# Attention and selection products on the full 128 x 128 array: operands of 4 to 64 rows, and results of 16 or 64 columns, widened with zeros

## The chip, the core and the metric

One core of a Trainium2 chip runs the whole program. The metric is the device time of one execution in microseconds (us); the lower, the better.

## The reference

Two transformer blocks on 512 tokens of 1024 features, in float32. Cut to what matters here:

```python
# block 1: forgetting attention (16 heads of 64) over 16 meta + 512 tokens, causal
logits = einsum('bhqd,bhkd->bhqk', qb, k) * scale + cb[..., None] - c[:, :, None, :]
p = softmax(where(allowed, logits, NEG)); y_a = einsum('bhqk,bhkd->bhqd', p, v)
# beside it retention: 4 heads, decayed scores, the same 16 + 512 keys; then gates, output products, SwiGLU

# block 2, two layers: neighbourhood attention (6 heads of 64: a window of the grid plus 256 context keys),
# grouped attention (6 query heads, 2 key heads of 64: 512 + 256 keys), a spatial gating unit, SwiGLU
s = concat([s_loc + bias, s_ctx], -1); p = softmax(s); o = p_loc @ v_win + p_ctx @ v_ctx
```

## The kernel before

Activations lie feature-major: a tile has 128 features on its 128 partitions and tokens along its columns. Where operands meet on TensorE they are pairs of float32r tiles (hi, lo) with hi + lo equal to the float32 value, and a product is made of three matmuls, hi hi, hi lo and lo hi (`mm3`, L296 to L303). A matmul takes a stationary operand (rows = what is summed over, columns = the rows of the result) and a moving one.

In the attention parts the head size is 64, half of the array's rows. A score is made of two matmuls instead of three. The first has all 128 rows: `A` holds the query's high part in 64 rows and its low part in the other 64, and `B1` holds the key's high part twice. The second has 64 rows: the query's high part against the key's low part, which lies in `B2`, one tile for both heads of a pair, in the head's own half:

```python
nc.tensor.matmul(ps[:, c:c + n], A[:, q], B1[:, c:c + n], start=True, stop=False)                  # L856
nc.tensor.matmul(ps[:, c:c + n], A[rows, q], B2[hp][rows, c:c + n], start=False, stop=True)        # L857
```

L856 and L857 are the forgetting attention (`fox`), L1476 and L1477 the neighbourhood attention (`na_streams`), L1655 and L1656 the grouped attention (`gqa`). After the scores come a maximum (VectorE), exponentials (ScalarE, into a tile `E`), transposes by TensorE (L892 in fox, L1330 in the other two), a split of the transposed tile in two (ScalarE writes `ph` at L322, then VectorE writes `pl` at L323), and the products with the values (L882 and L883; L1322). The other two add the reciprocal sums as a product with 64 result columns (L1339) in columns of the same bank.

Other operands with few rows: the meta tokens (16 keys: L882 and L883 with `VM`, the retention's `vmh` and `vml`) and constants that pick a row out of several (`esel`, `rsel`, `gsel`: 64 rows; L814, L815, L778 to L782, L1703). Results with 16 rows: transposes and scores of the 16 meta tokens.

The order of the work: generators are woven by a count of steps (`weave`), so that the projections of the next heads fill the attention of these; a scheduler then orders each engine's instructions, except GpSimd's, which keep the program's order. In block 2 an item of attention is 256 queries of one head; the scores of the next item go ahead of the sums of this one (`LOOK` is 1), and the values' product of a chunk of two key blocks comes one chunk after its transposes (`keysums`, L1311). Layer 0 has 18 items of either attention, layer 1 has 12. `E` has 5 buffers in the grouped attention and 6 in the neighbourhood attention (`EBUFS`, `NEBUFS`). While attention runs, GpSimd makes the low parts of the weights (`wlo`, L271).

Of the kernel before, what the change touches and what calls it, by code (L numbers as in the profile page):

```python
# [18 lines left out]
KD = 8  # L19
# [12 lines left out]
# buffers  # L32
# [21 lines left out]
# tiles added up before a sum over partitions  # L54
# [4 lines left out]
# steps (or columns of products) that lie between an operand and its use  # L59
# [8 lines left out]
# the pace of the work beside the products  # L68
# [11 lines left out]
# columns of the packed per-feature vectors  # L80
# [49 lines left out]
class Kern:  # L130
    """The program. Where operands meet on the tensor engine they are float32r pairs (hi, lo) with
    hi + lo exactly the float32 value, and a product is hi hi + hi lo + lo hi."""
# [51 lines left out]
    def weave(self, fill, main, ahead=1.0):  # L184
        """Run two generators side by side so that they end together (fill sooner by `ahead`). Their
        numbers of steps come from the first trace. main may ask for steps of fill in self.fill."""
        i = len(self.counted)
        self.counted.append(None)
        nf, nm = self.counts[i] if self.counts else (1, 1)
        self.fill = fill = Steps(fill)  # L190
        im = 0
        for _ in main:
            im += 1
            while fill.live and (fill.n + 1) * nm <= im * nf * ahead:
                fill.step()
        while fill.live:
            fill.step()
        self.counted[i] = (max(fill.n, 1), max(im, 1))

# [13 lines left out]
    def pump(self, cols):  # L213
        """Let the queue keep pace with a product of so many columns."""
# [59 lines left out]
    def prefetch(self, n):  # L274
        """Load the first units of weights."""
# [3 lines left out]
    def wunit(self, name, idx, k0=0, k1=KD, width=128):  # L279
        """The next unit of weights, [128, k1 - k0, width] in two parts; later units are set going."""  # L280
# [15 lines left out]
    def mm3(self, pss, wh, wl, xhs, xls, start, stop):  # L296
        """pss += W^T X with W and X each in two parts; lists run over chunks of columns."""
# [22 lines left out]
    def split(self, hi, lo, src):  # L320
        """hi + lo = src exactly."""
# [4 lines left out]
    def rsqrt(self, v, w, side=False):  # L326
        """1/sqrt(v) for v [128, w] (w <= 40), to float32; with side set mostly on an engine that has time."""
# [4 lines left out]
        # a guess from the exponent, a step of third order (without its factor c = 3/8), one of second order  # L332
# [39 lines left out]
    def affine(self, v, st, toks, col0, a, b):  # L372
        """v = a st + b in the rows that the token tiles have."""
# [14 lines left out]
    def bcasting(self, r, toks, ps=None):  # L388
        """r [token, tile] to a PSUM tile whose rows are all r, tokens along columns. A generator."""
# [60 lines left out]
    def until(cnt, n):  # L450
        """Wait until so many tiles have been set going."""
# [3 lines left out]
    def rms1(self, X, U, gname, c0, n, acc=NACC):  # L455
        """U[:, c0:c0+n] = RMS norm of X over features, split. A generator."""
# [164 lines left out]
    def gates(self, ff, tri, room, chl):  # L621
        """chl = cumulative log sigmoid of the forget gates ff [head, token], split over two row groups."""
# [21 lines left out]
        # log sigmoid z = min(z, 0) - log1p(e), e = exp(-|z|); log1p(e) = 2 atanh(e / (2 + e))  # L644
# [26 lines left out]
    def rounded(self, T, name, shape):  # L671
        """A constant of zeros and ones as float32r."""
# [5 lines left out]
    def foxconsts(self, X, fc):  # L678
# [4 lines left out]
        esel, rsel = self.rounded(T, "esel", [64, 16]), self.rounded(T, "rsel", [64, 256])  # L683
# [3 lines left out]
        chl = T([64, 528], "chl", 1, F32R)  # L687
# [5 lines left out]
    def fox(self, X, Y, fx, mask, esel, rsel, kq, chl):  # L693
# [4 lines left out]
        for i in range(2):  # L698
            rt = T([64, 528], f"rt{i}", 1, F32R)
            nc.gpsimd.memset(rt.bitcast(F32), 0.0)  # L700
            rts.append(rt)
        raw, ready = {}, {}

        def proj(hp, first=False):
            """Projections of a pair of heads and the mean squares of q and k."""
# [6 lines left out]
            def stat(u, c0, n, sq):  # L712
                st = self.at()
                toks = [(i, a, m) for i, (a, m) in enumerate(self.TOK1) if c0 <= a < c0 + n]
                for x, (i, a, m) in enumerate(toks):        # sums of squares per token and head
                    nc.tensor.matmul(st[:m, 2 * x:2 * x + 2], sq[:, a - c0:a - c0 + m], self.hsel, start=True, stop=True)
# [44 lines left out]
        def pair(hp):  # L761
            """The operands of a pair's attention: q and k normalised, v by tokens."""
# [3 lines left out]
            # 1 / rms per token and head, in columns (q h0, q h1, k h0, k h1) per token tile  # L766
# [20 lines left out]
            B2[hp] = T([128, 528], "B2", 2, F32R)  # L787
# [3 lines left out]
        def values(hp):  # L791
# [3 lines left out]
            for i, (c, n) in enumerate(self.TOK1):  # L795
                o = pt[:, (i - 1) * 128:i * 128] if i else ptm[:16, 0:128]
                nc.tensor.transpose(o, vs[:, c:c + n], ident)
            VT, VM = T([128, 4, 2, 2, 64], "VT", 2, F32R), T([16, 2, 2, 64], "VM", 2, F32R)
# [3 lines left out]
            nc.scalar.activation(VM[:, :, 0, :], pmv, AF.Copy)  # L802
            nc.vector.tensor_tensor(VT[:, :, :, 1, :], ptv, VT[:, :, :, 0, :].bitcast(F32), op=ALU.subtract)
            nc.vector.tensor_tensor(VM[:, :, 1, :], pmv, VM[:, :, 0, :].bitcast(F32), op=ALU.subtract)
# [3 lines left out]
        def head(x):  # L808
            """A head's q and k in two parts, and its biases."""
            hp, h = divmod(x, 2)  # L810
            # bias +c (the scores carry the opposite sign), and with the causal mask
            pcb = self.mm()
            es = esel[:, x:x + 1].to_broadcast([64, 128])
# [15 lines left out]
            nc.vector.tensor_tensor(B2[hp][rows], ks[rows], B1[rows].bitcast(F32), op=ALU.subtract)  # L829
# [5 lines left out]
        def scores(x):  # L835
            hp, h = divmod(x, 2)
            A, B1, cb, cbm = ready.pop(x)
            rows = slice(64 * h, 64 * h + 64)
# [9 lines left out]
            for i in range(4):  # L848
# [23 lines left out]
        def sums(x):  # L872
# [6 lines left out]
            def pv():  # L879
                j, kp, n, ph, pl = todo.pop(0)  # L880
                vv = (VT[:, j, h] if j >= 0 else VM[:, h]).rearrange("p a d -> p (a d)")
                nc.tensor.matmul(py[:, 512 - n:512], vv, ph[:kp, :n], start=j < 0, stop=False)  # L882
                nc.tensor.matmul(py[:, 512 - n:512], vv, pl[:kp, :n], start=False, stop=j == 3)  # L883

            for j in range(-1, 4):
                n = 512 - 128 * max(j, 0)
                kp = 128 if j >= 0 else 16
# [6 lines left out]
                self.split(ph[:kp, :n], pl[:kp, :n], pe[:kp, :n])  # L894
                todo.append((j, kp, n, ph, pl))
# [8 lines left out]

        normed, B2, V, Es = {}, {}, {}, {}
# [20 lines left out]
    def retgates(self, X, Y, hs):  # L926
        """silu(g) = g (1 + tanh(g / 2)) / 2, the half being in hcol"""
# [10 lines left out]
    def ret(self, X, Y, rp):  # L938
# [10 lines left out]

        def proj(h):  # L950
            dec, decm = T([128, 512], "dec", 1), T([16, 512], "decm", 1)
            nc.scalar.dma_start(out=dec, in_=I["decay"][h])
            nc.scalar.dma_start(out=decm, in_=I["decaym"][h])
# [17 lines left out]
            # values, token-major, centred over the head's features  # L971
# [12 lines left out]
            for d in range(2):  # L984
                for i, (c, n) in enumerate(self.TOK1):
                    o = ptv[:, i - 1, d * 128:(d + 1) * 128] if i else ptm[:16, d * 128:(d + 1) * 128]
                    nc.tensor.transpose(o, vss[d][:, c:c + n], self.ident)
# [1064 lines left out]
```

## Time and profile before

| | us |
|---|---|
| median of 3 runs (3511.92 to 3517.06) | 3514.89 |
| span of the profiled execution, first to last instruction | 3506.6 |
| fox, 436 to 775 of the span | 339 |
| attention of layer 0, 1687 to 1965 | 278 |
| attention of layer 1, 2765 to 3012 | 247 |

The median is 8.3 us above the profiled execution's span: what lies around the span, with the difference between executions. PE is TensorE's matmuls, PEld its weight loads, DVE VectorE, ACT ScalarE, POOL GpSimd. "64\*128" in a row of PE is a matmul with 64 rows and 128 columns of stationary operand, "64x256" its moving operand. Matmuls overlap, so the pace of a stream is read from one start to the next and not from a matmul's own duration. A product of plain float32 operands (transposes, L1339) stands as two records.

### The profile page before, as it was taken

How to read it: one execution, taken by the hardware profiler on the slowest of the kernel's cores; microseconds unless marked ns; L12 is line 12 of the kernel's file. 1: busy time of each engine (PE TensorE's matmuls, PEld its weight loads, DVE VectorE, ACT ScalarE, POOL GpSimd, SP SyncE). 2: the span in 40 equal slices, each digit the busy share in tenths (PEclk: the TensorE clock that was granted, in tenths of full speed). 3: DMA queues.
4: the chain of work that ended last, by engine and by line, in shares of the span. 5: the costliest groups of instructions: out<-in, count | busy, mean ns of one | idle time of the engine just before them, and what ended most of it. 6: DMA issues, size and time to landing. Idle time of an engine off the chain costs nothing. (4 is left out here: it accounts for less than half of the span.)

```text
span 3506.6 us, 50184 instructions
## 1 busy us (share of the span) xinstructions
PE 3365.7 (96%) x19680; PEld 2907.4 (83%) x19680; DVE 2083.9 (59%) x4419; ACT 1324.2 (38%) x2273; POOL 481.8 (14%) x443
## 2 busy tenths in 40 slices
PE   8999999999999999999999989999998999989998
PEld 7999977878788987889677878888898777878887
DVE  7983577776633769764766674222256666674335
ACT  4222345552323523234554443111234464452223
POOL 0000122223200110011211240000013111230001
PEclk9999999999999999999999899999999999899999
DMA  6663421122133656643001222212234201334233
GB/s 206 212 201 95 138 68 49 37 64 62 63 98 106 197 171 197 193 143 99 23 16 55 68 82 91 67 61 61 73 112 131 67 20 54 93 115 125 88 99 103
DMA packets 112205, 350.89 MB, mean 100 GB/s; under 512 B 12896, under 2 KB 26784, under 8 KB 111712
## 3 DMA queue, kind: packets, MB, share of 16 engines
q1 hardware_dynamic: 86464, 280.07, 25.8%
q10 hardware_dynamic: 25216, 65.51, 5.8%
q8 instruction: 155, 2.54, 0.3%
q0 software_dynamic: 288, 2.10, 0.2%
q14 instruction: 82, 0.67, 0.1%
HBM read 339.24 MB, written 8.39 MB: 99 GB/s over the span
## 5 line engine op out<-in xcount | busy, mean ns | idle before, releaser
L269 ACT ACTIVATE whi<-raw 128x1024 fp32r<-128x1024 f32 (+3 forms) x543 | 550.1, 1013 | 1434.6 <-PE mm L301 783.1
L300 PE MATMUL mm<-ah,whi 128*128 128x512 f32 (+3 forms) x2496 | 809.3, 331 | 15.3 <-ACT s L546 6.8
L301 PE MATMUL mm<-al,whi 128*128 128x512 f32 (+3 forms) x2496 | 788.1, 327 | 1.3 <-DVE al L1157 1.0
L271 DVE TENSOR_TENSOR wlo<-raw,whi 128x1024 fp32r<-128x1024 f32 (+2 forms) x464 | 557.1, 1203 | 352.3 <-ACT whi L269 349.1
L303 PE MATMUL mm<-ah,wlo 128*128 128x512 f32 (+3 forms) x2496 | 715.3, 328 | 3.6 <-DVE wlo L271 3.6
L300 PEld LDWEIGHTS mm<-ah,whi 128*128 128x128 f32 x2496 | 474.4, 190 | 68.8 <-ACT ah L1156 7.8
L301 PEld LDWEIGHTS mm<-al,whi 128*128 128x128 f32 x2496 | 474.0, 190 | 42.3 <-DVE al L1157 3.1
L300 PE MATMUL at<-ah,whi 128*128 128x512 f32 (+4 forms) x1368 | 482.4, 354 | 7.8 <-DVE B L1439 2.2
L301 PE MATMUL at<-al,whi 128*128 128x512 f32 (+4 forms) x1368 | 459.1, 336 | 0.1
L303 PE MATMUL at<-ah,wlo 128*128 128x512 f32 (+4 forms) x1368 | 456.6, 335 | 0.0
L303 PEld LDWEIGHTS mm<-ah,wlo 128*128 128x128 f32 x2496 | 430.2, 190 | 31.1 <-DVE wlo L271 4.8
L300 PE MATMUL mm<-gh,whi 128*128 128x256 f32 (+3 forms) x1168 | 376.9, 327 | 0.9 <-ACT gh L322 0.6
L301 PE MATMUL mm<-gl,whi 128*128 128x256 f32 (+3 forms) x1168 | 367.7, 324 | 0.7 <-DVE gl L323 0.7
L303 PE MATMUL mm<-gh,wlo 128*128 128x256 f32 (+3 forms) x1168 | 339.5, 324 | 0.0
L300 PEld LDWEIGHTS at<-ah,whi 128*128 128x128 f32 x1368 | 264.8, 194 | 41.2 <-issue 10.8
L301 PEld LDWEIGHTS at<-al,whi 128*128 128x128 f32 x1368 | 265.5, 194 | 23.2 <-issue 3.2
L303 PEld LDWEIGHTS at<-ah,wlo 128*128 128x128 f32 x1368 | 264.0, 193 | 21.7 <-issue 0.7
L1119 POOL TENSOR_TENSOR sq<-x,x 128x256 f32<-128x256 f32 (+1 forms) x68 | 73.8, 1097 | 1252.5 <-DVE x L1176 819.1
L300 PEld LDWEIGHTS mm<-gh,whi 128*128 128x128 f32 x1168 | 220.6, 189 | 23.9 <-ACT gh L322 0.9
L301 PEld LDWEIGHTS mm<-gl,whi 128*128 128x128 f32 x1168 | 220.6, 189 | 18.0 <-DVE gl L323 1.4
L271 POOL TENSOR_TENSOR wlo<-raw,whi 128x1024 fp32r<-128x1024 f32 (+1 forms) x79 | 180.1, 2287 | 376.3 <-ACT whi L269 347.7
L550 DVE TENSOR_TENSOR s<-s,mm 128x256 f32<-128x256 f32 (+3 forms) x142 | 72.1, 527 | 240.5 <-PE mm L303 239.1
(385 smaller groups left out, 4873.8 us busy)
## 6 DMA issues: line engine op xcount, KB each, us to landing
raw<-in_wfin SPq DMA_DIRECT2D x116, 512.0 KB, 3.6
raw<-in_win SPq DMA_DIRECT2D x115, 512.0 KB, 3.6
wm<-in_wmod ACTq DMA_DIRECT2D x96, 512.0 KB, 4.2
raw<-in_w2in SPq DMA_DIRECT2D x52, 512.0 KB, 4.3
raw<-in_w1in SPq DMA_DIRECT2D x50, 512.0 KB, 4.0
raw<-in_wfout SPq DMA_DIRECT2D x48, 448.0 KB, 3.3
raw<-in_w1out SPq DMA_DIRECT2D x24, 448.0 KB, 3.4
raw<-in_w2out SPq DMA_DIRECT2D x24, 448.0 KB, 3.4
```

What stands on the lines that cost most here:

```text
L269: self.nc.scalar.activation(hi, raw, AF.Copy)
L271: eng.tensor_tensor(lo, raw, hi.bitcast(F32), op=ALU.subtract)
L300: t.matmul(ps, wh, xh, start=start, stop=False)
L301: t.matmul(ps, wh, xl, start=False, stop=False)
L303: t.matmul(ps, wl, xh, start=False, stop=stop)
L550: nc.vector.tensor_tensor(s[:, c], s[:, c], ps[1][:, 512 * b:512 * b + n], op=ALU.mult)
L1119: nc.gpsimd.tensor_tensor(x, X[j][:, c], X[j + 1][:, c], op=ALU.add)
```

## The change

Every operand with few rows gets all 128, the rest being zeros. `B2` becomes a tile for each half (`B2[h]`), whose other half GpSimd sets to zero once: for all pairs in fox and in the grouped attention; for the pairs 0 and 1 in the neighbourhood attention, where pair 2 writes into the tiles of pair 0. `VM`, `vmh`, `vml` and the meta tokens' decay become tiles of 128 rows, set to zero once. `esel`, `rsel`, `gsel`, `rt` and `chl` get 128 rows. Transposes, scores and sums of squares of the 16 meta tokens take 128 columns (the meta tokens and the 112 after them), and the product at L1339 has 128 result rows. Layer 0 gets 4 buffers of `E` in either attention (5 and 6 before; layer 1 keeps them), `yt` has one buffer instead of two, and a tile of zeros became one column. The number of matmuls is the same, 19077 in either program; VectorE and ScalarE have as many instructions as before.

```diff
-EBUFS = 5
-NEBUFS = 6
+EBUFS = (4, 5)
+NEBUFS = (4, 6)
...
+        B2 = [T([128, 528], f"B2{h}", 1, F32R) for h in range(2)]
+        VMs = [T([128, 2, 2, 64], f"VM{i}", 1, F32R) for i in range(2)]
+        for h in range(2):
+            nc.gpsimd.memset(B2[h][64 - 64 * h:128 - 64 * h].bitcast(F32), 0.0)
+            nc.gpsimd.memset(VMs[h].bitcast(F32), 0.0)
...
-                    nc.tensor.matmul(ps[:, c:c + n], A[rows, q], B2[hp][rows, c:c + n], start=False, stop=True)
+                    nc.tensor.matmul(ps[:, c:c + n], A[:, q], B2[h][:, c:c + n], start=False, stop=True)
...
-                nc.tensor.matmul(py[:, 512 - n:512], vv, ph[:kp, :n], start=j < 0, stop=False)
-                nc.tensor.matmul(py[:, 512 - n:512], vv, pl[:kp, :n], start=False, stop=j == 3)
+                nc.tensor.matmul(py[:, 512 - n:512], vv, ph[:, :n], start=j < 0, stop=False)
+                nc.tensor.matmul(py[:, 512 - n:512], vv, pl[:, :n], start=False, stop=j == 3)
...
-                    nc.tensor.transpose(pe[:kp, q0:q0 + 128], E[:, k0:k0 + kp], ident)
+                    nc.tensor.transpose(pe[:, q0:q0 + 128], E[:, k0:k0 + 128], ident)
...
-                nc.tensor.matmul(py[0:64, 256 + 128 * t:384 + 128 * t], rs[:, t:t + 1].to_broadcast([128, 64]),
+                nc.tensor.matmul(py[:, 256 + 128 * t:384 + 128 * t], rs[:, t:t + 1].to_broadcast([128, 128]),
                                  self.ident, start=False, stop=False)
...
-        yt = T([64, 256], "yt", 2)
+        yt = T([64, 256], "yt", 1)
...
-            B2 = self.xp.tile([128, T2], F32R, name=self.nm("B2"), tag="x", bufs=KD)
+            if pr < 2:
+                lows.append([self.nb2() if pr == 1 else self.xp.tile([128, T2], F32R, name=self.nm("B2"), tag="x", bufs=KD)
+                             for _ in range(2)])
+                for h in range(2):
+                    nc.gpsimd.memset(lows[pr][h][rows[1 - h]].bitcast(F32), 0.0)
+            B2 = lows[pr % 2]
...
-                            nc.tensor.matmul(o, A[rows, q], B2[rows, k0:k0 + 256], start=False, stop=True)
+                            nc.tensor.matmul(o, A[:, q], B2[h][:, k0:k0 + 256], start=False, stop=True)
...
-        B2 = self.xp.tile([128, T2], F32R, name=self.nm("gB2"), tag="x", bufs=KD)
         B = [keep([128, T2], "gB1", 2, F32R) for _ in range(2)]
+        B2 = [keep([128, T2], "gB2", 2, F32R) for _ in range(2)]
+        for g in range(2):
+            nc.gpsimd.memset(B2[g][64 - 64 * g:128 - 64 * g].bitcast(F32), 0.0)
...
-                    nc.tensor.matmul(ps[:, c:c + n], A[rows, q], B2[rows, k0 + c:k0 + c + n], start=False, stop=True)
+                    nc.tensor.matmul(ps[:, c:c + n], A[:, q], B2[kv][:, k0 + c:k0 + c + n], start=False, stop=True)
```

TensorE's queue in the grouped attention of layer 0, before: a tile of 128 queries' scores, then transposes. In these rows the shape is that of the result; `gB_15504` is `B1`, `gB_15503` the `B2` that both key heads share.

```order
L300 MATMUL at_16748<-ah_12064,whi_16634 128x512
L1655 MATMUL mm_16758<-gB_15504,A_16612 128x512
L1656 MATMUL mm_16758<-gB_15503,A_16612 128x512
L1655 MATMUL mm_16758<-gB_15504,A_16612 128x256
L1656 MATMUL mm_16758<-gB_15503,A_16612 128x256
L1330 MATMUL at_16766<-c_ident,E_16719 128x128
```

The same place in the change, where `gB_15491` is the key head's own `B2`:

```order
L300 MATMUL at_16740<-ah_12050,whi_16626 128x512
L1666 MATMUL mm_16750<-gB_15489,A_16601 128x512
L1667 MATMUL mm_16750<-gB_15491,A_16601 128x512
L1666 MATMUL mm_16750<-gB_15489,A_16601 128x256
L1667 MATMUL mm_16750<-gB_15491,A_16601 128x256
L1336 MATMUL at_16758<-c_ident,E_16711 128x128
```

Nothing moved: the second product of each pair reads another tile, with 128 rows instead of 64.

GpSimd's queue at the start of fox, before; the adds at L441 belong to the norm of the second half of the tokens, which feeds the projections:

```order
L688 MEMSET chl_4898 64x528
L700 MEMSET rt_4903 64x528
L700 MEMSET rt_4905 64x528
L441 TENSOR_TENSOR sq_4927<-sq_4927 128x256
L441 TENSOR_TENSOR sq_4927<-sq_4927,sq_4940 128x256 x2
```

The same place in the change:

```order
L688 MEMSET chl_4898 128x528
L700 MEMSET rt_4903 128x528
L700 MEMSET rt_4905 128x528
L706 MEMSET B_4907 64x528
L707 MEMSET VM_4909 128x256
L706 MEMSET B_4908 64x528
L707 MEMSET VM_4910 128x256
L441 TENSOR_TENSOR sq_4935<-sq_4935 128x256
L441 TENSOR_TENSOR sq_4935<-sq_4935,sq_4948 128x256 x2
```

Four memsets have come ahead of the adds. In the same way three come at the start of the retention, and in each layer of block 2 two ahead of the adds of the norm before the projections (L1119), two in the projection of pair 0 and two in that of pair 1 of the neighbourhood attention.

## Rows read from the trace of the kernel before

**Rows 1.** The page: the span, and TensorE's busy time.

```profile
span 3506.6 us, 50184 instructions
PE 3365.7 (96%) x19680; PEld 2907.4 (83%) x19680; DVE 2083.9 (59%) x4419; ACT 1324.2 (38%) x2273; POOL 481.8 (14%) x443
```

**Rows 2.** Stages: busy PE, PEld, DVE, ACT, POOL; granted clock, DMA share, GB/s.

```profile
436.00:775.00 339.00, 332.58 (x1970) 265.45 (x1970) 252.37 (x768) 178.41 (x387) 85.94 (x46) 0.97 0.17 52
1687.00:1965.00 278.00, 267.47 (x1401) 202.34 (x1400) 173.03 (x396) 142.90 (x297) 40.52 (x59) 0.91 0.09 29
2765.00:3012.00 247.00, 237.35 (x1257) 180.62 (x1255) 159.49 (x359) 125.16 (x236) 38.83 (x40) 0.94 0.11 33
1930.00:1965.00 35.00, 34.25 (x118) 25.76 (x119) 16.78 (x55) 12.84 (x30) 1.54 (x1) 0.56 0.07 21
```

**Rows 3.** Timeline of PE, grouped attention, layer 0: start, duration (us), what.

```profile
1693.88 0.40 PE L300 MATMUL at<-ah,whi 128*128 128x512 f32 x1
1694.12 0.39 PE L1655 MATMUL mm<-gB,A 128*128 128x512 f32 x1
1694.43 0.49 PE L1656 MATMUL mm<-gB,A 64*128 64x512 f32 x1
1694.86 0.38 PE L1655 MATMUL mm<-gB,A 128*128 128x256 f32 x1
1695.17 0.38 PE L1656 MATMUL mm<-gB,A 64*128 64x256 f32 x1
1695.48 0.44 PE L1330 MATMUL at<-c_ident,E 128*128 128x128 f32 x2
```

**Rows 4.** The same timeline, values' products and transposes 3 us later.

```profile
1698.79 0.28 PE L1322 MATMUL at<-ph,VT 128*128 128x256 f32 x1
1698.90 0.29 PE L1322 MATMUL at<-pl,VT 128*128 128x256 f32 x1
1699.03 0.60 PE L1330 MATMUL at<-c_ident,E 128*128 128x128 f32 x4
1699.38 0.36 PE L1322 MATMUL at<-ph,VT 128*128 128x256 f32 x1
```

**Rows 5.** The same timeline around the reciprocal sums of an item.

```profile
1701.84 0.28 PE L1322 MATMUL at<-pl,VT 128*128 128x256 f32 x1
1702.05 0.65 PE L1339 MATMUL at<-c_ident,sm 128*64 128x128 f32 x4
1702.63 0.38 PE L1322 MATMUL at<-ph,VT 128*128 128x256 f32 x1
```

**Rows 6.** Timeline of PE in fox.

```profile
517.09 0.34 PE L856 MATMUL mm<-B,A 128*128 128x400 f32 x1
517.37 0.45 PE L857 MATMUL mm<-B,A 64*128 64x400 f32 x1
517.75 0.55 PE L892 MATMUL at<-c_ident,E 128*128 128x128 f32 x3
```

**Rows 7.** The lines with few rows or columns: count, duration min/median/max (ns), forms.

```profile
L1477 PE MATMUL mm<-B,A x108: 377/382/580, 1793.1 to 3012.9; 64*128 64x256 f32 x108
L1656 PE MATMUL mm<-gB,A x96: 379/490/792, 1687.8 to 2871.4; 64*128 64x512 f32 x48, 64*128 64x256 f32 x48
L1656 PE MATMUL at<-gB,A x12: 377/380/382, 1700.8 to 1799.0; 64*128 64x256 f32 x12
L857 PE MATMUL mm<-B,A x80: 273/389/502, 494.1 to 759.8; 64*128 64x144 f32 x16, 64*128 64x272 f32 x16, 64*128 64x400 f32 x16, 64*128 64x512 f32 x16
L1339 PE MATMUL at<-c_ident,sm x240: 272/273/476, 1702.1 to 3024.4; 128*64 128x128 f32 x120
```

**Rows 8.** The split after the transposes in layer 0: line, duration min/median/max (ns).

```profile
L322 ACT ACTIVATE ph<-at x67: 576/598/647, 1696.5 to 1956.8; 128x512 fp32r<-128x512 f32 x67
L323 DVE TENSOR_TENSOR pl<-at,ph x67: 671/691/694, 1697.2 to 1957.5; 128x512 fp32r<-128x512 f32 x67
```

**Rows 9.** Memsets on GpSimd by form: busy us, mean ns of one | idle before.

```profile
L1693 POOL MEMSET rt<- 64x768 f32 x4 | 2.9, 733 | 0.0
```

More of the change, by code (lines that the diff above doesn't have):

```diff
@@ L715, in stat @@
                 for x, (i, a, m) in enumerate(toks):
-                    nc.tensor.matmul(st[:m, 2 * x:2 * x + 2], sq[:, a - c0:a - c0 + m], self.hsel, start=True, stop=True)
+                    nc.tensor.matmul(st[:, 2 * x:2 * x + 2], sq[:, a - c0:a - c0 + 128], self.hsel, start=True, stop=True)
                 x = toks[0][0] == 0
@@ L795, in values @@
             for i, (c, n) in enumerate(self.TOK1):
-                o = pt[:, (i - 1) * 128:i * 128] if i else ptm[:16, 0:128]
-                nc.tensor.transpose(o, vs[:, c:c + n], ident)
-            VT, VM = T([128, 4, 2, 2, 64], "VT", 2, F32R), T([16, 2, 2, 64], "VM", 2, F32R)
+                o = pt[:, (i - 1) * 128:i * 128] if i else ptm[:, 0:128]
+                nc.tensor.transpose(o, vs[:, c:c + 128], ident)
+            VT, VM = T([128, 4, 2, 2, 64], "VT", 2, F32R), VMs[hp % 2]
             ptv = pt.rearrange("p (j h d) -> p j h d", j=4, h=2)
@@ L828, in head @@
             nc.vector.tensor_copy(B1[oth], B1[rows].bitcast(F32))
-            nc.vector.tensor_tensor(B2[hp][rows], ks[rows], B1[rows].bitcast(F32), op=ALU.subtract)
+            nc.vector.tensor_tensor(B2[h][rows], ks[rows], B1[rows].bitcast(F32), op=ALU.subtract)
             ready[x] = A, B1, cb, cbm
@@ L948, in ret @@
         state, gate = {}, {}
+        decm, vmh, vml = T([128, 512], "decm"), T([128, 256], "vmh", 1, F32R), T([128, 256], "vml", 1, F32R)
+        for t in (decm, vmh.bitcast(F32), vml.bitcast(F32)):
+            nc.gpsimd.memset(t, 0.0)
         def proj(h):
-            dec, decm = T([128, 512], "dec", 1), T([16, 512], "decm", 1)
+            dec = T([128, 512], "dec", 1)
             nc.scalar.dma_start(out=dec, in_=I["decay"][h])
-            nc.scalar.dma_start(out=decm, in_=I["decaym"][h])
+            nc.scalar.dma_start(out=decm[:16], in_=I["decaym"][h])
             QK = []
@@ L985, in proj @@
                 for i, (c, n) in enumerate(self.TOK1):
-                    o = ptv[:, i - 1, d * 128:(d + 1) * 128] if i else ptm[:16, d * 128:(d + 1) * 128]
-                    nc.tensor.transpose(o, vss[d][:, c:c + n], self.ident)
+                    o = ptv[:, i - 1, d * 128:(d + 1) * 128] if i else ptm[:, d * 128:(d + 1) * 128]
+                    nc.tensor.transpose(o, vss[d][:, c:c + 128], self.ident)
             mu = self.vcols(5)
@@ L997, in proj @@
             vch, vcl = T([128, 4, 256], "vch", 1, F32R), T([128, 4, 256], "vcl", 1, F32R)
-            vmh, vml = T([16, 256], "vmh", 1, F32R), T([16, 256], "vml", 1, F32R)
             self.split(vch, vcl, vc)
-            self.split(vmh, vml, vm)
-            state[h] = QK, (vch, vcl, vmh, vml), (dec, decm)
+            self.split(vmh[:16], vml[:16], vm)
+            state[h] = QK, (vch, vcl), dec
             yield
         def attend(h):
-            ((qh, ql), (kh, kl)), (vch, vcl, vmh, vml), (dec, decm) = state.pop(h)
+            ((qh, ql), (kh, kl)), (vch, vcl), dec = state.pop(h)
             SC = []
@@ L1243, in layer2 @@
                     self.napool = p
-                    tiles = [p.tile([128, T2], F32R, name=self.nm("nB1"), tag="nB1", bufs=2) for _ in range(2)]
-                    self.nb1 = lambda: tiles.pop()
+                    pairs = [[p.tile([128, T2], F32R, name=self.nm(t), tag=t, bufs=2) for _ in range(2)] for t in ("nB1", "nB2")]
+                    self.nb1, self.nb2 = (t.pop for t in pairs)
                     self.weave(fill(), attend(p), AHEAD[3])
@@ L1385, in na_streams @@
         Tl = self.maker(na)
-        zero = Tl([128, 256], "zero")
+        zero = Tl([128, 1], "zero")
         nc.gpsimd.memset(zero, 0.0)
@@ L1392, in na_streams @@
         state = {}
-        first = []
+        first, lows = [], []
         def load(pr, h, tile):
@@ L1437, in k @@
                     nc.scalar.activation(o, i, AF.Copy)
-                    o, i, hi = views(c0, B2[rows[h], c], ps[rows[h], :n], B1s[h][rows[h], c].bitcast(F32))
+                    o, i, hi = views(c0, B2[h][rows[h], c], ps[rows[h], :n], B1s[h][rows[h], c].bitcast(F32))
                     nc.vector.tensor_tensor(o, i, hi, op=ALU.subtract)
@@ L1485, in scores @@
                     nc.vector.tensor_tensor_reduce(
-                        out=E[:, 256:512], in0=ps[:, 256:512], in1=zero, scale=1.0, scalar=sm[:, t:t + 1],
+                        out=E[:, 256:512], in0=ps[:, 256:512], in1=zero.to_broadcast([128, 256]), scale=1.0, scalar=sm[:, t:t + 1],
                         op0=ALU.add, op1=ALU.max, accum_out=sm[:, 2 + t:3 + t])
@@ L1616, in main @@
                 nc.scalar.activation(B[g][rows], Q[3][rows], AF.Copy)
-                nc.vector.tensor_tensor(B2[rows], Q[3][rows], B[g][rows].bitcast(F32), op=ALU.subtract)
+                nc.vector.tensor_tensor(B2[g][rows], Q[3][rows], B[g][rows].bitcast(F32), op=ALU.subtract)
                 nc.vector.tensor_copy(B[g][oth], B[g][rows].bitcast(F32))
@@ L1646, in scores @@
                 i, kv, part = x
-                rows = slice(64 * kv, 64 * kv + 64)
                 if (i, kv) not in cur:
@@ L1932, in _constants @@
     C["causal"] = np.where(np.arange(128)[None, :] <= p, 0.0, BIG).astype(np.float32)
-    es = np.zeros((64, 16), np.float32)
+    es = np.zeros((128, 16), np.float32)
     es[np.arange(16), np.arange(16)] = 1
@@ L1938, in sel @@
     def sel(n):
-        m = np.zeros((64, n // 2, 128), np.float32)
+        m = np.zeros((128, n // 2, 128), np.float32)
         for r in range(n):
```

43 lines of the change are left out of this document (19 added, 24 removed).

## The prediction

> **What bounds the kernel now.** I read the page first: TensorE's matmuls are busy for 96% of the span and VectorE for 59% [rows 1]. So a change that shortens TensorE's stream can shorten the span, if the stage in which it does so has nothing else that is as long. I then cut out the three stages that hold the edited lines (with the first and last start of each line [rows 7]), and read who else is busy there: in fox VectorE 252 of 339 us, in the attention of layer 0 173 of 278, in that of layer 1 159 of 247; ScalarE has less in each [rows 2]. TensorE is busy 96 to 98%, so it sets the pace in all three. The third view is the timeline of TensorE alone, where the pace is the distance between starts. At the full array a product of 512 columns takes 0.24 us (1693.88 to 1694.12) [rows 3] and one of 256 columns 0.11 to 0.13, mean 0.12 [rows 4]. At a product of 64 rows that pace breaks on both sides.
>
> **What the change removes.** The step from a full product of 512 columns to its 64-row partner takes 0.31 us and the step out of that partner 0.43, where the pace is 0.24 each: 0.07 + 0.19 = 0.26 too much. For 256 columns it is 0.31 in and 0.31 out against 0.12: 0.38 too much [rows 3, 4]. The padded product has the form of its neighbours (128 rows and columns, float32r), so I give it their pace; a matmul's time depends on its columns in all these rows, and the columns stay. The sum over the lines [rows 7]:
> - 256 columns: 108 at L1477 and 48 + 12 at L1656, 168 x 0.38 = 64 us.
> - 512 columns: 48 at L1656 x 0.26 = 12.5 us.
> - Fox, 80 at L857: the product of 400 columns is entered after 0.28 and left after 0.38 us [rows 6]; at full pace 400 columns take about 0.19 (in between 0.12 and 0.24), so 0.28 too much, x 80 = 22 us.
> - L1339: 240 records are 120 products, two for each of 60 items. The step in takes 0.21 against 0.12, and the four records 0.58 us [rows 5], where four records of the same operand type on the full array take 0.35 [rows 4]: 0.09 + 0.23 = 0.32, x 60 = 19 us.
> - The rest, which I did not cost line by line: 32 products with `VM`, 24 in the retention, 32 + 24 + 13 with the selection constants, and the 16-column ones. Below, zero; above, the 0.28 [rows 6] for each of these 125, 35 us. They mostly stand in pairs, so that a pair shares one way in and out: I take half, 17 us.
>
> Together about 135 us of TensorE's time: fox 34 (22 + 12 of the rest), layer 0 with 96 products of 256 columns, 24 of 512 and 36 items 36.5 + 6 + 11.5 = 54, layer 1 with 72, 24 and 24 the same way 41, elsewhere 5.
>
> The Trainium skill (TensorEngine Tiling, section Key Properties) says that a change of tiling mode drains TensorE; the trace agrees that each change costs. With the 128 cycles that TensorE: Matmul & The Clock Gate (Part 2, step DRAIN) gives for a drain, an estimate of 0.053 us a change, some 830 changes (two for each of 296 products, 60 pairs at L1339 and some 60 groups of the rest) would cost 44 us; the rows say 0.07 to 0.19 for each, and the sum above goes by them.
>
> **How much of it stays.** Nothing here becomes as long as TensorE: after 34, 54 and 41 us are gone, VectorE is busy 252 of 305, 173 of 224 and 159 of 206 us (83, 77 and 77%). But work now comes sooner than its operands. In block 2 a chunk of two key blocks goes through transposes 0.60 us [rows 4], the copy on ScalarE 0.60 and the subtraction on VectorE 0.69 [rows 8], with hand-overs of about 0.1, so some 2.0 us from the first transpose until `pl` can be used, and that use comes a chunk later, after the next transposes. TensorE's own work in a chunk of the grouped attention is 4 transposed blocks 0.35 and 4 values' products 0.48 [rows 4], and two thirds of a tile's scores: 0.91 before (1694.12 to 1695.48 is 1.36 us [rows 3]), 0.48 after (0.24 + 0.24 + 0.12 + 0.12 is 0.72). So 1.74 us before and 1.31 after. To the use of `pl` one adds the next transposes and a product, 0.47: 2.2 before, longer than the 2.0, and 1.8 after, shorter by 0.2. Where no other work stands between, 0.2 of the 0.43 gained goes into a new wait for `pl`: about half is kept. Where projections fill in, all is. I take 70% for both layers, (54 + 41) x 0.7 = 66 us, 80% for fox, where every slot has products of projections but VectorE has the least room, 27 us, and the 5 elsewhere: 98 us. What is late next is `pl` (L323) and the copy ahead of it (L322).
>
> **The clock.** The granted clock is 0.56 in 1930 to 1965 and 0.91 and 0.94 over the two layers' attention [rows 2]. Since its two levels are 2.4 and 1.2 GHz, 0.91 over 278 us is 50 us at 1.2 GHz, and 0.94 over 247 is 30. In the slow stretch a matmul takes 35 / 118 = 0.30 us, in the whole stage 278 / 1401 = 0.20. So getting all 80 us back at the higher level would give some 27 us; nothing says that it comes back, and new waits could lower it elsewhere. Bounds 27 gained and as much lost; I take 6 gained, as a denser stream is nearer to what the engine does in the stretches at 2.4 GHz. The Trainium skill (TensorE: Matmul & The Clock Gate, Part 1) has activity release the throttle. By that rule all 27 would come, and the sum below would be 21 us larger; the trace shows the two levels, not the rule.
>
> **What the change adds.** 19 more instructions on GpSimd, all memsets but for the smaller tile of zeros. One of 768 columns takes 0.73 us [rows 9], so by columns 0.5 for 528 and 512, 0.25 to 0.35 for 256. Eight of 768 in the two layers, four in fox (1.7 us) and three in the retention make 9 us. GpSimd keeps its order, so behind them wait the adds of L441 in fox (1.7 us late) and those of L1119 at the start of either layer (1.5 each), on which norms and then projections wait; the memsets of pairs 0 and 1 stand ahead of a `wlo`, which is needed two units later. Between 0 and 9 us; I take 4, the places where a norm waits. The wider transposes and scores of the meta tokens keep their moving columns, so no time. One buffer of `yt`, written once in an item some 6 us long: nothing. Four buffers of `E` are what two items need, the one being summed and the one being scored: I take 1 us, and price the bad case below.
>
> Sum: 98 + 6 - 4 - 1 = 99, about 100 us. The profiled span of 3506.6 becomes 3407; with the 8.3 us between that span and the median, 3514.9 - 100 = **3415 us**.
>
> **Rivals.**
> - All of the 135 is kept and half of the clock comes back: 135 + 13 - 5 = 143, 3372 us. For it: VectorE and ScalarE have room in every stage [rows 2]. Against: the chain of 2.0 us.
> - The chain of split and products takes over in both layers and VectorE's bursts in fox: 30% kept, 135 x 0.3 = 40, 3475 us. For it: `pl` is 0.2 us late in a bare chunk already by the sum above, and the scores' own chain (maximum, exponentials) shares the two engines. Against: much of the time projections stand in between.
> - The change doesn't do what it says: the steps around a 64-row product are long for another reason, such as its operand's arrival, and the padded one is as slow. Then 3510 to 3520. Against it: the excess is the same 0.31 in at L1656 with 512 and 256 columns.
> - Slower: with 4 buffers in layer 0 the scores of an item can't go ahead until the last transposes of the item two before, so that each of the 3 chunks of 36 items waits for its whole chain. A chunk then loses up to 2.0 - 0.35 = 1.65 us, 36 x 3 x 1.65 = 178 us, and the time is 3415 + 178 = 3593. It decides from 100 / 108 = 0.93 us a chunk. Against: the transposes of an item are issued before the scores of the one after the next in either order.
>
> **How the numbers follow.** My forecast, a gain of 70 to 125 us (3390 to 3445), gets 0.55; all kept 0.20; mostly taken back 0.20; no effect 0.03; slower 0.02. The range leaves out about a tenth on either side: low 3370, the first rival's own value; high 3465, so that of the second rival the worse half is out. About 0.2% (7 us) is what a measurement of this kernel can tell from no change: faster 0.95, same 0.03, slower 0.02.
>
> **What would show it.** The steps around the padded products should be 0.24 and 0.12 us, and L1339's four records 0.35; if they aren't, the first sum is wrong. The three stages should be near 312, 240 and 218 us. TensorE should wait for `pl` and `ph` in the layers; if those waits are absent the gain is larger, if they exceed 40 us it is smaller. The granted clock of the layers should be 0.91 to 0.96. A wait of VectorE for a free `E` in layer 0 would be the slower rival's mark, and GpSimd's memsets ahead of L441 should delay the first sums of squares by under 2 us.

## The result and the profile after

The changed kernel takes 3389.0 us (median of 4 runs, 3385.7 to 3391.6) where the kernel before takes 3513.4 beside it: a ratio of 0.9641, 95% interval 0.9605 to 0.9678, 124 us. The forecast was 3415 in a range of 3370 to 3465. Between the two profiled executions the span falls by 3506.6 - 3385.9 = 120.7 us; the gains below are of these spans, where nothing else is said.

The page answers to [rows 1]: TensorE is still the engine that is busy, and the other engines do what they did, but for GpSimd's 19 new instructions.

```profile
span 3385.9 us, 50242 instructions
PE 3223.0 (95%) x19680; PEld 2875.9 (85%) x19680; DVE 2076.3 (61%) x4419; ACT 1321.3 (39%) x2273; POOL 491.3 (15%) x462
```

The stages of [rows 2] now take 305, 234 and 206 us, where 312, 240 and 218 were forecast. Their edges were found by setting the n-th matmul of one trace beside the n-th of the other. The columns are those of [rows 2].

```profile
436.00:741.00 305.00, 294.25 (x1968) 261.76 (x1969) 248.35 (x768) 177.87 (x387) 83.71 (x49) 0.98 0.17 54
1652.00:1886.00 234.00, 208.21 (x1401) 180.49 (x1401) 171.81 (x395) 142.11 (x297) 41.40 (x61) 0.98 0.11 34
2689.00:2895.00 206.00, 189.91 (x1253) 164.03 (x1253) 157.41 (x359) 124.55 (x236) 39.82 (x42) 0.99 0.13 40
```

Three things stand in these rows. The granted clock of the layers' attention has gone from 0.91 and 0.94 to 0.98 and 0.99, above the 0.91 to 0.96 of the forecast. TensorE's idle time in layer 0 has grown from 10.5 us (278 - 267.5) to 25.8 (234 - 208.2), in layer 1 from 9.7 to 16.1: part of what the products gave up is now waiting. And VectorE, busy 248 of 305 us in fox, has not become the bound.

The steps themselves are seen in the timeline of TensorE (start, duration, what; the lines of the edited products are now L1667, L1487, L861 and L1345). These are rows of the grouped attention, of fox and of the reciprocal sums, which answer to [rows 3, 6, 5]:

```profile
1659.27 0.40 PE L300 MATMUL at<-ah,whi 128*128 128x512 f32 x1
1659.50 0.39 PE L1666 MATMUL mm<-gB,A 128*128 128x512 f32 x1
1659.73 0.39 PE L1667 MATMUL mm<-gB,A 128*128 128x512 f32 x1
1659.95 0.28 PE L1666 MATMUL mm<-gB,A 128*128 128x256 f32 x1
1660.07 0.28 PE L1667 MATMUL mm<-gB,A 128*128 128x256 f32 x1
1660.19 0.38 PE L1336 MATMUL at<-c_ident,E 128*128 128x128 f32 x2
...
514.42 0.34 PE L860 MATMUL mm<-B,A 128*128 128x400 f32 x1
514.60 0.34 PE L861 MATMUL mm<-B,A 128*128 128x400 f32 x1
514.78 0.49 PE L896 MATMUL at<-c_ident,E 128*128 128x128 f32 x3
...
1665.87 0.61 PE L1345 MATMUL at<-c_ident,sm 128*128 128x128 f32 x4
1666.23 0.36 PE L1328 MATMUL at<-ph,VT 128*128 128x256 f32 x1
```

The padded products run at their neighbours' pace: 0.23 us at 512 columns, 0.12 at 256, 0.18 at 400, 0.36 for the four sums, where [rows 3, 5, 6] had 0.31 to 0.43, 0.31, 0.28 and 0.38, and 0.58.

### The profile page after: what moved, and what is told of

It is laid out like the page before. It is cut to its first block, busy times and chain, and to the rows that moved or that the text cites. A ratio compares the mean times of both kernels' runs of the same rounds, so it can differ in the third digit from the quotient of the medians.

```text
span 3385.9 us, 50242 instructions
## 1 busy us (share of the span) xinstructions
PE 3223.0 (95%) x19680; PEld 2875.9 (85%) x19680; DVE 2076.3 (61%) x4419; ACT 1321.3 (39%) x2273; POOL 491.3 (15%) x462
## 5 line engine op out<-in xcount | busy, mean ns | idle before, releaser
L303 PEld LDWEIGHTS at<-ah,wlo 128*128 128x128 f32 x1368 | 265.2, 194 | 21.5 <-issue 0.5
```

Source lines behind the costliest of these rows:

```text
L303: t.matmul(ps, wl, xh, start=False, stop=stop)
```

## The experiments

Every kernel below was run beside the kernel before on the same chip; its time is a median, its ratio is to the kernel before. A "change of shape" is a place in TensorE's program where a product uses another part of the array (rows x columns) than the one ahead of it; they were counted in the program: 972 in the kernel before, 89 in the changed one.

Most gains below are also parted by the clock. Two traces are laid side by side, the n-th matmul of one beside the n-th of the other, and the differences of the steps from one matmul to the next are added up by the granted clock. "At full clock" is what stands in steps that had 2.4 GHz in both traces; "by the clock" is what came or went in steps that had 2.4 GHz in one and 1.2 in the other, a few us of the shapes' own with it. This split is good to some 5 us: between the two executions of run 10's kernel, and between the kernel before and run 7, whose products are the same, either part comes to between 3 and 6 us.

**1. The scores alone back at 64 rows.** In the changed kernel, at L1487, and likewise at L861 and L1667:

```diff
-nc.tensor.matmul(o, A[:, q], B2[h][:, k0:k0 + 256], start=False, stop=True)
+nc.tensor.matmul(o, A[64 * h:64 * h + 64, q], B2[h][64 * h:64 * h + 64, k0:k0 + 256], start=False, stop=True)
```

> The changed kernel with the three score products of the keys' low parts (L861, L1487, L1667) back at 64 rows; sums, selection products, meta tokens and buffers stay padded, and the order of instructions on every engine is that of the changed kernel. Theory (TensorE pays for each change of a product's tile shape; 296 products of 64 rows bring back 589 of the 883 changes that went): the steps out of these products are 0.3 to 0.4 us again, and of the gain of 124 us some 85 to 105 are lost (gross 64 + 12.5 + 22 = 98.5), so 3475 to 3495 us. Rival 1 (the selection products, the sums and the meta tokens carry more than their 37 us): under 75 lost, below 3465. Rival 2 (much of the gain is the clock that a stream without breaks is granted): more than 105 lost, and the time at 1.2 GHz back from 156 to over 190 us.

3470.4 us, ratio 0.9895 (0.9853 to 0.9936): 81 us of the 124 are lost by the times, 89 by the two ratios. By the times that is 4 below the theory's range and 6 above the first rival's, by the ratios it is inside the theory's. In the spans it is 82.5 us: 65.5 at full clock and 16.4 by the clock. The second rival's time at 1.2 GHz (189 us against over 190) and its loss (over 105) do not come, the first by 1 us, but a fifth of the loss is of its kind. The rest, 35 to 43 us, is what the sums, the selection products, the meta tokens and the clock of these give together.

**2. The sums alone padded**, in the kernel before:

```diff
-nc.tensor.matmul(py[0:64, 256 + 128 * t:384 + 128 * t], rs[:, t:t + 1].to_broadcast([128, 64]),
+nc.tensor.matmul(py[:, 256 + 128 * t:384 + 128 * t], rs[:, t:t + 1].to_broadcast([128, 128]),
```

> The kernel before with one edit alone: the product that spreads the reciprocals beside the sums (L1339) writes 128 columns of the array instead of 64. 120 changes of shape fewer. Theory: 0.32 us an item, 60 items, 19 us gross, of which 14 to 20 are kept: 3494 to 3500 us. Rival (the chain of split and products takes most of it back in the layers): 3 to 10 kept, 3504 to 3511.

3491.8 us, ratio 0.9941 (0.9915 to 0.9968): 11 to 30 us, middle 21, and a time 2 us below the theory's range; in the spans 15.8, all of it at full clock. The sum's 19 us for this line holds, and nearly all of it is kept.

**3. No padding, other order.** In the kernel before, products of 128 rows first and then those of 64; for the grouped attention:

```diff
 for c, n in chunks:
     nc.tensor.matmul(ps[:, c:c + n], A[:, q], B[kv][:, k0 + c:k0 + c + n], start=True, stop=False)
+for c, n in chunks:
     nc.tensor.matmul(ps[:, c:c + n], A[rows, q], B2[rows, k0 + c:k0 + c + n], start=False, stop=True)
```

and for the neighbourhood attention the same over the four pairs of a pair of blocks.

> The kernel before, with no product padded: in layers 0 and 1 the score products of an item or tile run by shape, first all of 128 rows, then all of 64 rows. All 365 products of 64 rows stay, and 215 changes of shape go. Theory (the change of shape costs): 72 ways in and out less at 256 columns x 0.38 = 27 us and 37 at 0.26 to 0.38 = 12, less up to 0.10 us for each of the 109 products that now follow one of 64 rows (11 us), so 28 to 39 us gross and 20 to 36 kept: 3478 to 3494 us. Rival (a product of 64 rows is slow by itself, whatever stands before it): the steps inside a group are 0.31 us as well, and the time is 3514 within 7 us.

3456.9 us, ratio 0.9853 (0.9817 to 0.9889): 52 us (51 in the spans). This decides against the rival, as all 365 products of 64 rows are still there and do the same work: it is the change of shape that costs, not the product of 64 rows. The gain is above the theory's 20 to 36 too, but only 28.3 us of it stand at full clock, inside that range; 21.6 came by the clock, for which the theory had no term.

**4. Pairs**, in the neighbourhood attention of the kernel before alone: for each block of 128 queries both products of 128 rows, then both of 64.

> The kernel before, with the neighbourhood scores of each block of 128 queries in the order two products of 128 rows, two of 64 (before: 128, 64, 128, 64; the kernel with all shapes grouped: four and four). The grouped attention keeps the order of before. 87 changes of shape go, no product is padded. Theory A (a change costs 0.09 us where the products beside it share a shape and 0.19 where shapes alternate): an item of 8 products pays 4 x 0.09 instead of 8 x 0.19, 1.16 us less, 24 items, 28 us: 3481 to 3489 us. Theory B (every change costs the same 0.19): 0.76 us less an item, 18 us: 3492 to 3499 us.

3481.3 us, ratio 0.9930 (0.9910 to 0.9951): 25 us, 27 in the spans. The median lies in theory A's range, but by luck: at full clock the gain is 14.3 us, nearer to B's 18, and 10.5 came by the clock. The rows of single items decide. An item's eight products in three orders, from the timelines of TensorE; first alternating (the kernel of run 1), where the eight take 1804.05 - 1801.56 = 2.49 us:

```profile
1801.56 0.36 PE L1486 MATMUL mm<-nB,A 128*128 128x256 f32 x1
1801.86 0.38 PE L1487 MATMUL mm<-B,A 64*128 64x256 f32 x1
1802.17 0.39 PE L1486 MATMUL mm<-nB,A 128*128 128x256 f32 x1
...
1803.74 0.38 PE L1487 MATMUL mm<-B,A 64*128 64x256 f32 x1
1804.05 0.39 PE L1328 MATMUL at<-ph,nVT 128*128 128x256 f32 x1
...
1804.69 0.33 PE L300 MATMUL at<-ah,whi 128*128 128x256 f32 x1
```

In pairs, 1898.28 - 1896.66 = 1.62 us:

```profile
1896.66 0.40 PE L1477 MATMUL mm<-nB,A 128*128 128x256 f32 x2
1896.98 0.50 PE L1479 MATMUL mm<-B,A 64*128 64x256 f32 x2
1897.41 0.50 PE L1477 MATMUL mm<-nB,A 128*128 128x256 f32 x2
1897.85 0.50 PE L1479 MATMUL mm<-B,A 64*128 64x256 f32 x2
1898.28 0.66 PE L1330 MATMUL at<-c_ident,E 128*128 128x128 f32 x4
```

And grouped (run 3), 1898.72 - 1897.50 = 1.22 us:

```profile
1897.50 0.62 PE L1479 MATMUL mm<-nB,A 128*128 128x256 f32 x4
1898.06 0.73 PE L1481 MATMUL mm<-B,A 64*128 64x256 f32 x4
1898.72 0.66 PE L1330 MATMUL at<-c_ident,E 128*128 128x128 f32 x4
```

Eight steps at 0.12 would be 0.96. So the surplus of these items is 1.53 us for 8 changes, 0.66 for 4 and 0.26 for 2; by the medians of the nine or ten such items that ran wholly at 2.4 GHz (2.40, 1.62 and 1.26 us) it is 1.44, 0.66 and 0.30. Theory A foresaw 0.36 for the pairs and B 0.76.

The single steps say where it sits. By the medians at full clock, a step from a product of 256 columns to the next product takes 0.12 us with no change of shape on either side, 0.21 if the next product has another shape, 0.22 if the one ahead had, and 0.31 with both. These four values are the same within 0.005 us in the kernel before and in runs 1, 3 and 4, wherever they occur. So at 256 columns a change has one price, 0.09 us in the step that leads into it and 0.10 in the step behind it, 0.19 together, as theory B had it. An item counted to its last product's end leaves out the step behind its last change: 8 x 0.09 + 7 x 0.10 = 1.42, 4 x 0.09 + 3 x 0.10 = 0.66 and 2 x 0.09 + 0.10 = 0.28.

The weight loads show where the time goes. First run 1, then the changed kernel:

```profile
1801.54 0.19 PEld L1486 LDWEIGHTS mm<-nB,A 128*128 128x128 f32 x1
1801.86 0.18 PEld L1487 LDWEIGHTS mm<-B,A 64*128 64x128 f32 x1
...
1764.84 0.19 PEld L1487 LDWEIGHTS mm<-B,A 128*128 128x128 f32 x1
1764.96 0.19 PEld L1486 LDWEIGHTS mm<-nB,A 128*128 128x128 f32 x1
```

In the changed kernel the load for the product at 1764.96 starts at 1764.84, with the product ahead of it. At a change of shape it starts only with its own product, at 1801.86 (0.002 us ahead in the median of 294 such products of the kernel before, after the loads had stood idle for 0.13 us). The 0.31 of the alternating step is then the load's 0.19 and the product's 0.12, one behind the other. In pairs and groups the load behind such a product starts 0.11 us after it and the next product another 0.12 later, which makes the 0.22. This is read from the timing; no run changed the loads alone. The Trainium skill (TensorEngine Tiling, Key Properties) says that a change of mode drains the engine and gives no price; the rows agree that every change costs, and the 0.19 is more than three times the 0.053 us that the prediction estimated from the skill.

**5. Both: grouped, and the sums padded**, in the kernel before.

> The kernel before with the scores of the layers grouped by shape and the spreading of the reciprocals at 128 columns, still with no padded key. Theory (the costs of changes add up): 52 + 20 = 72 us, 3438 to 3446 us. Rival (the two edits gain the same idle time, or a chain on the other engines becomes the bound): 50 to 60 us, 3451 to 3461 us.

3446.7 us, ratio 0.9829 (0.9802 to 0.9856): 60 us by the ratio, 62 in the spans. The times do not decide: the median is 1 us above the theory's range (3438 to 3446), while 60 us is the most that the rival allows. At full clock the gains add up: 42.7 us here, against 28.3 + 15.8 = 44.1 in runs 3 and 2. The clock gave 18.8 here, 21.6 in run 3 and took 2.3 in run 2.

**6. The changed kernel in the grouped order**, where the order leaves all shapes alike.

> The changed kernel with its scores in the grouped order, where every product has one shape in either order. Theory (grouping helped the kernel before by its shapes alone): no gain, 3385 to 3394 us. Rival (part of the 52 us came from the order itself, by weights that stay or by scores that come sooner): 8 us or more faster, below 3381 us, and then it is the fastest kernel.

3385.2 us, ratio 0.9659 (0.9636 to 0.9682), the changed kernel's own time. The order by itself gives nothing, so run 3 did not gain by its order.

**7. The buffers alone**, in the kernel before:

```diff
-EBUFS = 5
-NEBUFS = 6
+EBUFS = (4, 5)
+NEBUFS = (4, 6)
...
-yt = T([64, 256], "yt", 2)
+yt = T([64, 256], "yt", 1)
```

> The kernel before with the changed kernel's buffers alone: 4 instead of 5 and 6 buffers of the exponentials in layer 0 (5 instead of 6 would not have mattered in layer 1, which keeps its own), 1 instead of 2 of the sums' tile. Theory: no change, 3513 within 4 us. Rival (the fewer buffers hold back the scores of the next item): over 5 us slower, with VectorE waiting for a free tile of exponentials in layer 0; by the bound of the prediction up to 178 us.

3506.3 us, ratio 0.9990 (0.9967 to 1.0013): no difference, though 3 us below the theory's 3509, since the kernel before itself took 3511.3 beside it. VectorE waits for no free tile of exponentials, and ScalarE 1.0 us in all for one. The slower rival falls.

**8. A later `pl`**, in the changed kernel, behind the split of a chunk:

```diff
 self.split(ph, pl, pe)
+nc.vector.tensor_tensor(pl[:, 0:256], pe[:, 0:256], ph[:, 0:256].bitcast(F32), op=ALU.subtract)
```

> The changed kernel with half of the subtraction that makes the lower part of the transposed exponentials done twice (L323, 256 of 512 columns again, 132 chunks in the two layers), so that pl is some 0.4 us later in every chunk; the result is the same. Theory (the chain of transposes, copy and subtraction has slack, since other products stand between): under 10 us slower, 3389 to 3399 us. Rival (the chain of the prediction is already 0.2 us too long in a bare chunk): 132 x 0.4 x 0.5 to 1, 26 to 53 us slower, 3415 to 3442 us, with TensorE waiting for pl.

3410.5 us, ratio 0.9730 (0.9705 to 0.9754): 21.5 us slower than the changed kernel, between the two ranges, so both missed; beside run 6, measured with it, it is 25. The added subtraction takes 0.416 us, 54 us over 132 chunks, and 40% or more of that reaches the end. In the spans it is 24.3 us, 14.2 at full clock and 9.1 by the clock. The edit lengthens the chain and gives VectorE 54 us more work in one, so that which of the two costs the 14 us is not parted.

**9. The split in halves**, in the changed kernel:

```diff
-self.split(ph, pl, pe)
+for a in (0, 256):
+    self.split(ph[:, a:a + 256], pl[:, a:a + 256], pe[:, a:a + 256])
```

> The changed kernel with the copy and the subtraction of a chunk (L322, L323) made in two halves of 256 columns, so that the first key block's ph and pl are ready some 0.5 us sooner, for 0.15 us more of VectorE and 0.2 more of ScalarE in each of 132 chunks. Theory (the chain from the transposes to pl is what TensorE waits for in the layers, as 0.4 us more of it cost 0.17 us a chunk): 0.05 to 0.12 us less a chunk, 6 to 15 us faster than the changed kernel, 3374 to 3383 us, and TensorE's waits for ph and pl at least halved. Rival (VectorE and ScalarE themselves are short of time, and their 46 us more push the rest back): 0 to 15 us slower, 3389 to 3404 us.

3411.3 us, ratio 0.9716 (0.9692 to 0.9739): 22 us slower, outside both ranges, so both missed; in the spans 22.9, of it 14.8 at full clock. The edit did not do what it was meant to. ScalarE's copies of halves, grouped by line (count | busy, mean ns | idle before, by releaser):

```profile
L322 ACT ACTIVATE ph<-at 128x256 fp32r<-128x256 f32 x264 | 95.0, 383 | 72.5 <-PE at L1336 36.3 <-DVE pl L323 32.9 <-ACT E L1671 0.6
```

It waits 32.9 us for `pl`: in 99 of the 132 chunks the second copy starts only when VectorE has subtracted the first half. Where that is so, the second `pl` is ready after about 2 x (0.38 + 0.42) = 1.60 us where the whole one took 0.60 + 0.69 = 1.29, an estimate of 0.3 us later, and the run costs what run 8 costs.

The four kernels that keep or lengthen this chain, by the waits of TensorE's weight loads at the values' products (us in total, times, longest). Run 1, the changed kernel, run 8, run 9:

```profile
PEld at L1328 <- ACT ph L322: 5.1, 11, 1.0
PEld at L1328 <- DVE pl L323: 3.6, 8, 0.8
```

```profile
PEld at L1328 <- DVE pl L323: 11.6, 28, 1.0
PEld at L1328 <- ACT ph L322: 10.1, 25, 1.2
```

```profile
PEld at L1328 <- DVE pl L1339: 21.8, 42, 1.4
PEld at L1328 <- ACT ph L322: 4.5, 11, 1.0
```

```profile
PEld at L1328 <- ACT ph L322: 19.1, 40, 2.5
PEld at L1328 <- DVE pl L323: 15.8, 30, 4.0
```

8.7 us with 64-row scores, 21.7 without them, 26.3 and 34.9 with a later `pl`. What such a wait does to a gain is seen in one item. It is the one shown above for run 1, now in the changed kernel:

```profile
1764.76 0.36 PE L1486 MATMUL mm<-nB,A 128*128 128x256 f32 x1
1764.96 0.28 PE L1487 MATMUL mm<-B,A 128*128 128x256 f32 x1
...
1765.67 0.28 PE L1487 MATMUL mm<-B,A 128*128 128x256 f32 x1
1766.35 0.39 PE L1328 MATMUL at<-ph,nVT 128*128 128x256 f32 x1 [0.40 <-DVE pl L323]
...
1767.59 0.33 PE L1328 MATMUL at<-ph,nVT 128*128 128x128 f32 x1 [0.50 <-ACT ph L322]
1767.75 0.34 PE L300 MATMUL at<-ah,whi 128*128 128x256 f32 x1
```

The eight products now start within 0.91 us (2.18 before). From the first of them to the next projection it is 1767.75 - 1764.76 = 2.99 us, and in run 1 1804.69 - 1801.56 = 3.13: of the 1.27 us between the two, 0.14 are kept here, since the values' products wait for `pl` and then for `ph`.

**10. The changed kernel once more**, beside run 9.

> The changed kernel itself, beside the run above on the same chip: 3385 to 3394 us, 119 to 128 us faster than before, by any theory; it shows how far a second execution's time at 1.2 GHz differs from the first one's 156 us.

3389.1 us, ratio 0.9650 (0.9627 to 0.9674), span 3386.5. It spends 139 us at 1.2 GHz and the first execution 156, at the same span. (These sums take the last stretch to its end, some 2 us behind the last instruction, in all kernels alike.)

## Why the prediction was right, and which term was wrong

The forecast's direction, its mechanism and its range held; 120.7 us of span instead of 99 is mostly a matter of one term: of the 22 us between them the clock has 15 and the costs about 4.

**The removed steps.** All three pace figures came out as put (0.24, 0.12 and 0.35 against 0.23, 0.12 and 0.36). Run 3 shows that it is the change of shape that is paid for, so "no effect" is out. The sum that the scores made of it, 98.5 us, is 104 when the steps of the same places before and after are subtracted by their medians at full clock, and 89 by their means, which hold new waits too. The 0.38 for a pair of changes at 256 columns is twice the 0.19 that the rows of run 4 give.

**What was kept.** Parted by the clock as above, steps at 2.4 GHz in both traces gave 92.8 us; steps at 1.2 GHz before and 2.4 after gave 53.6; steps at 2.4 before and 1.2 after took 26.3; the rest is 0.9. In the 424 steps of the second kind, the shapes' own share at the rate of their stage is about 6, so the shapes gave 99 us, where the forecast had 98 before its costs. With run 7's trace in the place of before, whose products have the same shapes, it is 90 + 5 = 95. That the total fits is partly luck. By stage, and by the same sums, fox kept 31 of 34 us (forecast 27), layer 1 32 of 41 (29), layer 0 only 25 of 54 (38), and 11 (6 against run 7) lie elsewhere (5). What holds layer 0 back is read from TensorE's waits there, in an idle time that grew from 10.5 to 25.8 us. These are rows of them (us in total, times, longest), first before, 1687 to 1965, then after, 1652 to 1886:

```profile
PE at L1322 <- DVE pl L323: 1.6, 2, 0.9
PE at L1322 <- ACT ph L322: 0.7, 1, 0.7
PE mm L1655 <- ACT E L1659: 1.4, 1, 1.4
...
PE at L1328 <- DVE pl L323: 3.0, 7, 0.6
PE at L407 <- DVE pl L323: 2.9, 1, 2.9
PE at L1328 <- ACT ph L322: 1.9, 4, 0.7
PE at L1336 <- ACT E L1670: 1.8, 4, 0.5
PE mm L1666 <- ACT E L1670: 1.4, 2, 0.9
```

Waits for `pl` and `ph` came as named, but they are 5.5 of the 15 us that came on (2.3 before, 7.8 after); 3.4 are waits for the exponentials `E` (2.1 before, 5.5 after, smaller rows with them), and the rest are smaller ones for VectorE. So the mechanism was right and not alone. The 70% for layer 0 was too high, the half that the prediction gave a chunk "where no other work stands between" was nearer.

**The clock: the mis-sized term.** "I take 6 gained" is the term that was too small. It gave 53.6 - 6 - 26.3 = 21 us, and 27 against run 7's trace. In layer 0 alone it is 20, net: the stretch at 0.56 of [rows 2] is gone. The reason that was given, that a denser stream is nearer to the stretches at 2.4 GHz, is not in the rows: in that slow stretch TensorE was busy for 34.25 of 35 us, 98%, and in its whole stage 96%. The stretches granted at 1.2 GHz come to 203 us of the span before, and to 156 and 139 in two executions after. By number of changes, the kernels stand like this:

```
changes of shape      us at 1.2 GHz
972, 972, 885, 852    203, 220, 187, 223    (before, runs 7, 4, 2)
757, 678, 637         166, 189, 168         (runs 3, 1, 5)
89, 89, 89, 85, 91    156, 139, 171, 166, 156  (after, runs 10, 6, 8, 9)
```

That fewer changes go with less time at 1.2 GHz is shown, in the large and not from row to row; that they are the cause is not, as in no run one of the two was changed alone. What the clock costs can be read without any edit. Every execution has its mean granted clock, and with two levels 2 x (1 - clock) x span is its time at 1.2 GHz. Over the 39 executions of the kernel before this runs from 175 to 261 us, and on one chip each us of it goes with 0.42 us of span (standard error 0.03); most of the spread of this kernel's times, 3492 to 3533 us, goes with the clock. The means are 214 us before and 143 over eight executions of the changed kernel, so an estimate of 71 x 0.42 = 30 us for the clock's part; for run 3 (159 us) it is 23 of its 52. The Trainium skill (TensorE: Matmul & The Clock Gate, Part 1) has activity release the throttle, and by it the prediction put all 27 us of the layers' stages; the two layers' stages gave 19.6 + 8.8 = 28 by these sums, so its size was right there and mine wrong. In the rest of the span the clock took back 7. Most of that is a new stretch at 1.2 GHz where no edited product stands, at the start of layer 1:

```profile
2638.00:2648.00 10.00, 9.36 (x60) 8.89 (x60) 8.34 (x22) 6.17 (x12) 0.00 (x0) 0.99 0.08 14
2648.00:2669.00 21.00, 21.00 (x96) 19.90 (x96) 4.90 (x13) 5.69 (x9) 4.72 (x2) 0.51 0.37 120
```

A matmul is running all through it, at 0.22 us a matmul, and the same matmuls take 9.6 us less in the kernel before. 77 of 91 of them are of 128 columns, in steps of 0.12 us at 2.4 GHz. Whether that is activity in the sense of the rule, no run tells, so the trace neither bears it out here nor refutes it. It stands in the profiles of the changed kernel, both times, and of runs 1, 5, 6, 8 and 9, and not in those of runs 2, 3, 4 and 7. What decides it stays open.

**The costs.** Of the 4 us for memsets about 1 came, of the 1 for buffers nothing. The memsets take what was said (0.73 us at 768 columns, 0.54 at 528, 0.31 at 256). In fox the adds of L441 start 1.7 us later behind them, and the first sums of squares wait for these adds 2.29 us where it was 1.43; by 494 us of the span the matmuls stand again within 0.3 us of where they stood. At the norms of the layers the waits for GpSimd are the same (7.5 us before, 7.4 after). Run 7 has no loss by buffers. At L1720 in layer 0 one wait for VectorE's `q` is 5.6 us where it was 2.9.

**The rivals.** "All kept and half the clock" (3372) was nearer on the clock, 13 us, and had the share wrong; "taken back" (3475) had the mechanism of layer 0, its scores' own chain included, but not of the rest. The slower one fell with run 7.

## What to carry to other kernels

Where products of different shape on the array alternate, count the changes and read the steps in and out from the timeline: each change cost 0.19 us here, where a product of 256 columns takes 0.12. Zeros up to the full shape take the changes away, and a mere regrouping of the same products takes many of them, for no memory (52 us here, about 30 by the shapes and 20 by the clock). Before counting such a gain, follow the operands of what comes next: chains on other engines that just fit the old pace take the gain back, in layer 0 half of it. And keep the clock apart in both traces when a size is judged: 21 of these 121 us were not the products' own, and run 4's time agreed with the wrong theory by the clock.

## What the runs showed that was not expected

- Half of the price of a change of shape falls on the step behind it: inside pairs, a step without a change took 0.22 us, as long as one with a change, since its weight load started 0.11 us into the step and not before it.
- A product of 64 rows behind others of 64 rows takes 0.12 us for 256 columns in the median, the pace of the full array.
- Two executions of one kernel spent 156 and 139 us at 1.2 GHz and differed by 0.6 us in span, although over many executions the span follows the clock: between their matching steps the clock gave 14.9 - 10.8 = 4 us, and the steps at 2.4 GHz in both lost 5.
